# A fixed instruction order for the first layer's modulation and norms

## The chip, the cores and the metric

The kernel runs on one core of a Trainium2 chip. The metric is the device time of one execution in microseconds. The kernel before took 2765.76 us (median of three runs, 2760.23 to 2770.64). The engines are TensorE (PE; its weight loads are listed as PEld), VectorE (DVE), ScalarE (ACT), GpSimd (POOL) and SyncE (SP, which issues the DMA loads here).

## The reference, cut to what matters

Two layers of an attention and mLSTM block are followed by a second block. The change concerns the start of the first layer only. There x is the latent sequence (1024 rows of 1024) and ctx the context (256 rows of 1024):

```
sc, scc = silu(c), silu(c_ctx)
mod_x = split((sc  @ w_ada[l] + b_ada[l]), 3)     # shift, scale, gate of the latents
mod_c = split( scc @ w_ada[l] + b_ada[l] , 3)     # shift, scale, gate of the context
xn = rmsnorm(x,   norm_g) * (1 + scale_x) + shift_x
cn = rmsnorm(ctx, norm_g) * (1 + scale_c) + shift_c
aq, ak, av, ... = split(xn @ w_in)                # the same for cn
```

So before the first projection can run, 1024 x 2048 weights of w_ada (the shift and scale thirds, 8 MB in fp32) are multiplied with two vectors, and ten tiles of 128 rows are normed, transposed (features on the partitions) and modulated. The gate third comes later.

## The kernel before, in words

Rows are handled in tiles of 128: tiles 0 to 7 are x, 8 and 9 are ctx. `start` (L513) does the work described above; `phase_a` (the first projections and the attention) follows it and multiplies in the order context first (values and keys of tiles 8 and 9), then tiles 0 to 3, then 4 to 7. Its weights are loaded into the ring `rraw` (two places at the start of the arena `fa`), and split on ACT (L265) and DVE (L266).

*Rows.* `load` (L523) fetches one tile into a place of `rx`, ten places of 1024 columns in the arena `ta`. `scale` squares the row on ACT with a running sum (L469), makes the factor on DVE (L462) and POOL (L464, a power of -1/2), and multiplies in place on DVE (L531).

*Modulation vectors.* `ada(l, j)` (L421) is a generator over h, the four quarters of 256 columns; j=1 is scale, j=0 shift. `ada_rows` (L394) loads w_ada in two pieces of 512 rows (512 KB each) through a ring of five places, and multiplies them with the two vectors: 8 products of 128x256 each into one PSUM bank (L416), two hardware records a product. DVE copies the 2x256 result into the row tile `ar` (L418), of which there is one; four small products turn it into columns (L429); DVE adds b_ada into `AB` (L435), and for the scale makes (1+scale)*norm_g (L438).

*Norm.* `norm(t, h)` (L533) takes tiles t and t+1 and feature blocks 2h and 2h+1: four transposes into one PSUM buffer (L542), then the modulation straight out of PSUM into `z` (i=0 on DVE, L547; i=1 on ACT, L545), then `split` (L248): a rounded copy on ACT (L249) and the remainder on DVE (L250). There are three PSUM buffers for transposes and columns (`pt`, banks 2 to 4), and five for products (`pg`).

*What sets the order.* The lines are not issued as they are written. A scheduler places instructions on the engines by their priority (their order in the text) and its own model of time, over a block that reaches from the setup to the end of the second layer's mixers; each engine then executes its list in order. Only the last part of the program (`feed_forward`, L1990) is written in `manual_schedule`. Within such a region each engine issues the region's instructions in the order of the text; where they fall among instructions from outside the region stays with the scheduler.

Of the kernel before, what the change touches and what calls it, by code (L numbers as in the profile page):

```python
# [9 lines left out]
AF = mybir.ActivationFunctionType  # L10
ALU = mybir.AluOpType
# [176 lines left out]
FO, FS, TS = 2176, 9752, 11008  # L188


class Kernel:
# [50 lines left out]
    def mm3(self, out, lh, ll, rh, rl, start, stop):  # L242
        mm = self.nc.tensor.matmul
        mm(out, lh, rh, start=start, stop=False)  # L244
        mm(out, lh, rl, start=False, stop=False)  # L245
        mm(out, ll, rh, start=False, stop=stop)  # L246
# [58 lines left out]
    def gemm_n(self, w, kk, t, n, x=None, pg=None, ks=range(8), p=None, stop=True):  # L305

        start, p = p is None, p or (pg or self.pg).get()
        X, L = x or (self.xh, self.xl)
        g, o = (t // 4, (t % 4) * 128) if t < 8 else (2, (t - 8) * 128)
        for k in ks:  # L310
            xh, xl = X[g][:, k, o:o + 128], L[g][:, k, o:o + 128]
            h, l = w[k // kk]
            self.mm3(p[:, :n], xh, xl, h[:, k % kk], l[:, k % kk], start and k == ks[0], stop and k == ks[-1])
        if not stop:
            return p
        self.bg.step(self.rate)
        self.bg2.step()
        return p
# [5 lines left out]
    def columns(self, rows, name):  # L324

        nc = self.nc
        r = self.rraw.get([128, 128])
        o = 0
        for ap in rows:
            n = ap.shape[0]  # L330
            nc.sync.dma_start(r[o:o + n], ap)
            o += n
        p = self.pt.get()
        nc.tensor.transpose(p[:, :o], r[:o], self.ident[:o, :o])
        v = self.const([128, o], name)
        nc.vector.tensor_copy(v, p[:, :o])
        return v
# [175 lines left out]
    def start(self):  # L513

        nc, V = self.nc, self.nc.vector
        self.xh, self.xl = [None] * 3, [None] * 3
        for g in range(3):
            self.new_xn(g)
        self.phase(F32)
        rx = self.T(0, 1024, 10)  # L520
        rows = {}

        def load(t):  # L523
            src = self.A["x"][0, t * 128:(t + 1) * 128] if t < 8 else self.A["ctx"][0, (t - 8) * 128:(t - 7) * 128]
            rows[t] = x = rx.get()
            nc.sync.dma_start(x.ap, src)

        def scale(t):
            x = rows[t]
            r = self.row_rstd(x.ap, self.rny.get().ap)  # L530
            V.tensor_scalar(x.ap, x.ap, r, None, op0=ALU.mult)  # L531

        def norm(t, h):  # L533

            p = self.pt.get()
            pv = p.re("p (k n) -> p k n", k=2)
            A = self.mod(0, t)
            z = self.rnz.get([128, 2, 256])
            for i in range(2):
                for j in range(2):  # L540
                    k = 2 * h + i
                    nc.tensor.transpose(pv[:, i, j * 128:(j + 1) * 128], rows[t + j][:, k * 128:(k + 1) * 128], self.ident)  # L542
                a, b = A(k)
                if i:
                    nc.scalar.activation(z[:, i], pv[:, i], AF.Identity, scale=a, bias=b)  # L545
                else:
                    V.tensor_scalar(z[:, i], pv[:, i], a, b, op0=ALU.mult, op1=ALU.add)  # L547
            g, o = (t // 4, (t % 4) * 128) if t < 8 else (2, (t - 8) * 128)
            self.split(self.xh[g][:, 2 * h:2 * h + 2, o:o + 256], self.xl[g][:, 2 * h:2 * h + 2, o:o + 256], z.ap)

        first = [8, 9, 0, 1, 2, 3]
        for t in first:
            load(t)
        rada = Ring(self.fa, [FO + 1024, FO + 2048] + [FO + 4628 + 1024 * i for i in range(3)], 1024)
        a, b = self.ada(0, 1, rada), self.ada(0, 0, rada)
        for h in range(4):
            next(a)
            next(b)
            if h == 0:
                for t in first:  # L560
                    scale(t)
            for t in (8, 0, 2):
                norm(t, h)
        for t in range(4, 8):
            load(t)
        self.late_constants()
        for t in (4, 6):
            scale(t)
            scale(t + 1)
            for h in range(4):  # L570
                norm(t, h)


    def rings_attention(self):
# [1751 lines left out]
```

## Time and profile before

| what | us |
|---|---|
| median of three runs | 2765.76 |
| the profiled execution's own time | 2766.28 |
| its span | 2764.5 |
| PE busy | 2618.6 |
| DVE busy | 1865.3 |
| ACT busy | 1451.2 |
| first product with w_ada starts | 16.50 |
| last group of columns (L429) starts | 58.94 |
| last split of tiles 2 and 3 ends | 70.20 |

Times in the views are microseconds from the start of the span. An engine's busy time counts its instructions; a matmul's duration is longer than the distance to the next one, since matmuls are pipelined, so rates are read from the starts of consecutive groups. In the view in order of time a row is a group of equal instructions in sequence: start, duration of the group, engine, line, operation, output<-inputs, shapes, count, and in brackets the idle time before it with what ended that.

### The profile page before, as it was taken

The numbers are of one execution on the slowest core, as the hardware profiler recorded it, in microseconds if no ns is written. First come the engines' busy times: TensorE is split into PE (matmuls) and PEld (weight loads), VectorE is DVE, ScalarE is ACT, GpSimd is POOL, SyncE is SP. The second block draws the span as 40 slices with busy tenths as digits, with TensorE's granted clock in tenths as the row PEclk, the third lists the DMA queues.
The fourth block names the chain that finished last, engine by engine and source line by source line (L and its number), as shares of the span: only waits on it lengthen the run. The fifth ranks groups of instructions, "written<-read, shape, count | busy, mean of one in ns | idle before, by whom it ended". The sixth has DMA issues, their size and how long they took to land. (4 is left out here: it accounts for less than half of the span.)

```text
span 2764.5 us, 43667 instructions
## 1 busy us (share of the span) xinstructions
PE 2618.6 (95%) x16222; PEld 2273.1 (82%) x16222; DVE 1865.3 (67%) x3758; ACT 1451.2 (52%) x3035; POOL 477.6 (17%) x686
## 2 busy tenths in 40 slices
PE   7999999999899999999998989899899999999998
PEld 3888888899789887878987878778788878888887
DVE  4788756636755788765456467987844477868978
ACT  4666645646632666555455153468833644753344
POOL 0122213413300022213223030025410000000000
PEclk9999999999999999999999989999989999999999
DMA  7001111111564202022113451423242576698846
GB/s 252 25 19 49 35 49 38 55 53 47 156 199 151 81 18 59 24 61 62 44 54 115 156 171 64 128 80 96 82 126 85 184 222 214 199 326 286 282 136 213
DMA packets 302817, 324.73 MB, mean 117 GB/s; under 512 B 17968, under 2 KB 242572, under 8 KB 302348
## 3 DMA queue, kind: packets, MB, share of 16 engines
q1 hardware_dynamic: 302604, 321.95, 37.0%
q8 instruction: 127, 2.08, 0.3%
q14 instruction: 86, 0.70, 0.1%
HBM read 274.86 MB, written 47.03 MB: 116 GB/s over the span
## 5 line engine op out<-in xcount | busy, mean ns | idle before, releaser
L244 PE MATMUL psum<-xa 128*128 128x512 f32 (+2 forms) x2136 | 755.3, 354 | 11.4 <-ACT xa L249 3.5
L246 PE MATMUL psum<-xa 128*128 128x512 f32 (+2 forms) x2136 | 747.2, 350 | 5.1 <-DVE xa L2076 3.4
L245 PE MATMUL psum<-xa 128*128 128x512 f32 (+2 forms) x2136 | 749.2, 351 | 1.6 <-DVE xa L266 1.5
L244 PEld LDWEIGHTS psum<-xa 128*128 128x128 f32 x2136 | 408.0, 191 | 65.2 <-ACT xa L249 4.8
L246 PEld LDWEIGHTS psum<-xa 128*128 128x128 f32 x2136 | 407.5, 191 | 56.1 <-DVE xa L2076 5.6
L245 PEld LDWEIGHTS psum<-xa 128*128 128x128 f32 x2136 | 407.8, 191 | 50.6 <-DVE xa L266 2.2
L464 POOL TENSOR_TENSOR rsb<-rsa,half 128x1 f32<-128x1 f32 (+2 forms) x125 | 89.2, 713 | 1010.2 <-DVE rsa L462 935.7
L244 PE MATMUL psum<-xa,xg 128*128 128x256 f32 (+1 forms) x864 | 248.4, 287 | 1.8 <-DVE fa L1522 1.2
L245 PE MATMUL psum<-xa,xg 128*128 128x256 f32 (+1 forms) x864 | 246.1, 285 | 0.0
L246 PE MATMUL psum<-xa,xg 128*128 128x256 f32 (+1 forms) x864 | 245.8, 284 | 0.0
L2074 ACT ACTIVATE xa<-t816a 128x1024 fp32r<-128x1024 f32 x122 | 126.1, 1056 | 186.1 <-PE psum L245 101.8
L265 ACT ACTIVATE xa<-fa 128x1024 fp32r<-128x1024 f32 (+1 forms) x104 | 109.9, 1059 | 196.5 <-PE psum L246 98.6
L266 DVE TENSOR_TENSOR xa<-fa,xa 128x1024 fp32r<-128x1024 f32 (+1 forms) x94 | 115.3, 1229 | 135.4 <-ACT xa L265 124.9
L2076 DVE TENSOR_TENSOR xa<-t816a,xa 128x1024 fp32r<-128x1024 f32 x122 | 146.0, 1221 | 78.6 <-ACT xa L2074 78.4
L805 POOL TENSOR_SCALAR fa<-fa,esk 128x640 f32<-128x640 f32 (+2 forms) x144 | 112.1, 791 | 451.3 <-DVE esk L803 349.7
L244 PEld LDWEIGHTS psum<-xa,xg 128*128 128x128 f32 x864 | 163.9, 190 | 3.2 <-DVE fa L1522 1.6
L245 PEld LDWEIGHTS psum<-xa,xg 128*128 128x128 f32 x864 | 163.9, 190 | 0.8 <-issue 0.7
L246 PEld LDWEIGHTS psum<-xa,xg 128*128 128x128 f32 x864 | 163.6, 189 | 0.4 <-issue 0.3
L244 PE MATMUL psum<-xg,xa 128*128 128x512 f32 x376 | 153.3, 409 | 2.9 <-DVE fa L1764 1.8
L246 PE MATMUL psum<-xg,xa 128*128 128x512 f32 x376 | 152.3, 405 | 1.0 <-POOL xa L266 1.0
L245 PE MATMUL psum<-xg,xa 128*128 128x512 f32 x376 | 152.5, 405 | 0.2 <-DVE xg L250 0.2
L1008 DVE SCALAR_TENSOR_TENSOR fa<-fa,vec 128x640 f32<-128x640 f32 (+2 forms) x128 | 110.4, 869 | 52.0 <-ACT fa L1006 42.4
(511 smaller groups left out, 5880.1 us busy)
## 6 DMA issues: line engine op xcount, KB each, us to landing
t816a<-in_w_down_dram SPq DMA_DIRECT2D x72, 512.0 KB
fa<-in_w_in_dram SPq DMA_DIRECT2D x64, 512.0 KB
t816a<-in_w_up_dram SPq DMA_DIRECT2D x64, 512.0 KB
fa<-in_w_ada_dram SPq DMA_DIRECT2D x48, 512.0 KB
t816a<-hd SPq DMA_DIRECT2D x36, 512.0 KB
fa<-in_w_up_dram SPq DMA_DIRECT2D x32, 512.0 KB
fa<-in_w_out_dram SPq DMA_DIRECT2D x24, 512.0 KB
fa<-in_w_down_dram SPq DMA_DIRECT2D x24, 512.0 KB
```

The lines of the kernel that those rows point to most:

```text
L244: mm(out, lh, rh, start=start, stop=False)
L245: mm(out, lh, rl, start=False, stop=False)
L246: mm(out, ll, rh, start=False, stop=stop)
L265: self.nc.scalar.activation(h.ap, r.ap, AF.Copy)
L266: (self.nc.gpsimd if self.wpool else self.nc.vector).tensor_tensor(l.ap, r.ap, h.ap.bitcast(F32), op=ALU.subtract)
L464: self.nc.gpsimd.tensor_tensor(r, e, self.half.broadcast_to([128, m]), op=ALU.pow)
L805: nc.gpsimd.tensor_scalar(P[j][:, :nk], P[j][:, :nk], e[:, j:j + 1], 0.0, op0=ALU.mult, op1=ALU.add)
L1008: nc.vector.scalar_tensor_tensor(y, U[i][:, lo + tap:hi + tap], col(tap), y, op0=ALU.mult, op1=ALU.add)
L2074: nc.scalar.activation(h.ap, r.ap, AF.Copy)
L2076: V.tensor_tensor(l.ap, r.ap, h.ap.bitcast(F32), op=ALU.subtract)
```

## The change

The lines of `start` that prepared tiles 8, 9 and 0 to 3 go into a new function, `start_first`, written in `manual_schedule`. In it:

- w_ada's pieces (units, in the order h, then scale before shift, then the two halves of the rows) get 13 places instead of 5: four places of `rx` that tiles 4 to 7 will take later, the five of before, the two of `rraw`, and the two of `z`. Thirteen loads are issued right behind the six rows; the last three when units 4, 5 and 6 have been multiplied; then tiles 4 to 7, and at the end the late constants.
- Each pair of rows is transposed as soon as it is scaled (`turn`), and copied from PSUM back into its own place, on ACT for odd h and on DVE for even h. Tiles 8, 9, 0 and 1 are turned ahead of the first product, tiles 2 and 3 between the first four units.
- The columns of a row `ar` (`columns`) are made behind the first unit of the next row. When the shift of a quarter is there, the three pairs are modulated in place, from SBUF, and split.

`spare` is the four places of `rx` (columns 6144 on of `ta`); `products(n, p)` multiplies unit n (four products, eight records) and, for n of 4 to 6, issues one more load. Tiles 4 to 7 are handled as before, outside the region.

```diff
-        first = [8, 9, 0, 1, 2, 3]
-        for t in first:
-            load(t)
-        rada = Ring(self.fa, [FO + 1024, FO + 2048] + [FO + 4628 + 1024 * i for i in range(3)], 1024)
-        a, b = self.ada(0, 1, rada), self.ada(0, 0, rada)
-        for h in range(4):
-            next(a)
-            next(b)
-            if h == 0:
-                for t in first:
-                    scale(t)
-            for t in (8, 0, 2):
-                norm(t, h)
-        for t in range(4, 8):
-            load(t)
-        self.late_constants()
+        with self.tc.manual_schedule():
+            self.start_first(rows, load, spare)
...
+        slots = spare
+        slots.extend(Ring(self.fa, [FO + 1024, FO + 2048] + [FO + 4628 + 1024 * i for i in range(3)], 1024))
+        slots.extend(Ring(self.fa, [0, 1088, FO + 7700, FO + 8724], 1024))
+        units = [(h, j, k) for h in range(4) for j in (1, 0) for k in (0, 4)]
...
+        def turn(t, h):
+            p = self.pt.get()
+            pv = p.re("p (k n) -> p k n", k=2)
+            for i in range(2):
+                for j in range(2):
+                    k = 2 * h + i
+                    nc.tensor.transpose(pv[:, i, j * 128:(j + 1) * 128], rows[t + j][:, k * 128:(k + 1) * 128], self.ident)
+            o = both(t, h)
+            if h % 2:
+                nc.scalar.activation(o, pv, AF.Copy)
+            else:
+                V.tensor_copy(o, pv)
...
+        def columns(h, j, r):
+            t = self.pt.get()
+            for i in range(2):
+                mm(t[:, 2 * i:2 * i + 2], r[0:2, i * 128:(i + 1) * 128], self.sel[0:2, 0:2], start=True, stop=True)
...
+            V.tensor_tensor(o, t[:, 0:4].rearrange("p (k a) -> p k a", a=2), b, op=ALU.add)
+            if j == 1:
...
+                return
+            for t in (8, 0, 2):
+                A = self.mod(0, t)
+                x, g, o = both(t, h), t // 4, (t % 4) * 128
+                for i in range(2):
+                    a, b = A(2 * h + i)
+                    if i:
+                        nc.scalar.activation(x[:, i], x[:, i], AF.Identity, scale=a, bias=b)
+                    else:
+                        V.tensor_scalar(x[:, i], x[:, i], a, b, op0=ALU.mult, op1=ALU.add)
+                self.split(self.xh[g][:, 2 * h:2 * h + 2, o:o + 256], self.xl[g][:, 2 * h:2 * h + 2, o:o + 256], x)
...
+        for t in (8, 9, 0, 1, 2, 3):
+            load(t)
+        for _ in range(13):
+            fetch()
+        slots.i += 4
+        sq = [square(8), square(9)]
+        for x in sq:
+            scaled(*x)
+        sq = [square(0), square(1)]
+        for h in range(4):
+            turn(8, h)
+        for x in sq:
+            scaled(*x)
+        sq = [square(2), square(3)]
+        for h in range(4):
+            turn(0, h)
+        for x in sq:
+            scaled(*x)
+        last = None
+        for n in range(0, 16, 2):
+            h, j, _ = units[n]
+            p = self.pg.get()
+            products(n, p)
+            if n < 4:
+                turn(2, n)
+            if last:
+                columns(*last)
+            products(n + 1, p)
+            if n < 4:
+                turn(2, n + 1)
+            r = self.s([5, 256], "ar256", 1)
+            V.tensor_copy(r[0:2], p[:2, :256])
+            last = h, j, r
+            if n == 6:
+                for t in range(4, 8):
+                    load(t)
+        columns(*last)
+        self.late_constants()
```

## Rows read from the trace of the kernel before

**Rows 1.** The page: busy time of PE, share of the span, instructions

```profile
PE 2618.6 (95%) x16222; PEld 2273.1 (82%) x16222; DVE 1865.3 (67%) x3758; ACT 1451.2 (52%) x3035; POOL 477.6 (17%) x686
```

**Rows 2.** Busy time in stretches (length; each engine's busy time, count; granted clock; DMA)

```profile
16.50:59.47 42.97, 42.97 (x198) 17.54 (x198) 19.46 (x50) 15.40 (x27) 2.70 (x5) 1.00 0.80 258
59.47:70.20 10.73, 9.34 (x68) 8.01 (x68) 7.44 (x12) 6.73 (x11) 0.00 (x0) 1.00 0.62 195
```

**Rows 3.** Waits of SP and of PE: total us, times, longest

```profile
SPq L405 <- PE psum L416: 16.6, 9, 3.6
...
PE psum L416 <- DMA fa<-in_w_ada_dram: 4.5, 1, 4.5
...
PE psum L1208 <- DVE t474a L1204: 5.8, 2, 5.5
```

**Rows 4.** PE in order of time, the modulation stage

```profile
11.51 0.48 PE L542 MATMUL psum<-ident,t1a 128*128 128x128 f32 x1 [1.00 <-DVE t1a L531]
16.50 6.98 PE L416 MATMUL psum<-fa,cc 128*2 128x256 f32 x20 [4.51 <-DMA fa<-in_w_ada_dram]
...
34.83 2.32 PE L416 MATMUL psum<-fa,cc 128*2 128x256 f32 x10
37.08 0.66 PE L542 MATMUL psum<-ident,t1a 128*128 128x128 f32 x4
37.67 0.59 PE L416 MATMUL psum<-fa,cc 128*2 128x256 f32 x2
38.19 0.60 PE L429 MATMUL psum<-sel,ar 2*128 2x2 f32 x4
38.72 0.59 PE L416 MATMUL psum<-fa,cc 128*2 128x256 f32 x2
...
58.94 0.60 PE L429 MATMUL psum<-sel,ar 2*128 2x2 f32 x4
```

**Rows 5.** Stretches, transposes of L542 alone (PE busy, count; weight loads)

```profile
16.40:59.47 43.07, 7.67 (x38) 3.87 (x38) 1.00 0.80 258
...
70.20:82.00 11.80, 4.21 (x22) 2.49 (x22) 1.00 0.18 50
```

**Rows 6.** ACT in order of time

```profile
12.42 1.06 ACT L469 ACTIVATE fa<-t1a 128x1024 f32<-128x1024 f32 x1
...
41.56 0.56 ACT L545 ACTIVATE fa<-psum,AB 128x256 f32<-128x256 f32 x1 [0.22 <-ACT fa L545]
42.02 0.62 ACT L249 ACTIVATE xc<-fa 128x512 fp32r<-128x512 f32 x1
```

**Rows 7.** DVE in order of time

```profile
13.81 0.15 DVE L462 TENSOR_SCALAR rsa<-nss 128x1 f32<-128x1 f32 x1
14.69 0.75 DVE L531 TENSOR_SCALAR t1a<-t1a,rsb 128x1024 f32<-128x1024 f32 x1 [0.73 <-POOL rsb L464]
...
42.67 0.69 DVE L250 TENSOR_TENSOR xc<-fa,xc 128x512 fp32r<-128x512 f32 x1
43.28 0.68 DVE L250 TENSOR_TENSOR xa<-fa,xa 128x512 fp32r<-128x512 f32 x1
43.89 0.54 DVE L547 TENSOR_SCALAR fa<-psum,AB 128x256 f32<-128x256 f32 x1
...
58.46 0.41 DVE L418 COPY ar<-psum 2x256 f32<-2x256 f32 x1 [0.78 <-PE psum L416]
59.58 0.16 DVE L435 TENSOR_TENSOR AB<-psum,vec 128x4 f32<-128x4 f32 x1 [0.71 <-PE psum L429]
...
69.52 0.68 DVE L250 TENSOR_TENSOR xa<-fa,xa 128x512 fp32r<-128x512 f32 x1
```

**Rows 8.** Nearest shapes: a group's mean ns, and L1588's min/median/max

```profile
L606 ACT ACTIVATE fa<-psum 128x512 f32<-128x512 f32 x20 | 11.8, 592 | 14.1 <-PE psum L246 14.0
...
L1541 DVE TENSOR_SCALAR t604a<-psum,hln 128x512 f32<-128x512 f32 x4 | 3.2, 806 | 4.3 <-ACT fa L1540 4.3
...
L1588 DVE TENSOR_SCALAR fa<-fa,sst x8: 349/820/2068, 1874.0 to 1957.2; 128x256 f32<-128x256 f32 x8
```

More of the change, by code (lines that the diff above doesn't have):

```diff
@@ L519, in start @@
         self.phase(F32)
-        rx = self.T(0, 1024, 10)
+        rx, spare = self.T(0, 1024, 10), self.T(6144, 1024, 4)
         rows = {}
@@ L571, in start, with start_first, fetch, square @@
                 norm(t, h)
+    def start_first(self, rows, load, spare):
+        nc, V = self.nc, self.nc.vector
+        mm = nc.tensor.matmul
+        slots = spare
+        slots.extend(Ring(self.fa, [FO + 1024, FO + 2048] + [FO + 4628 + 1024 * i for i in range(3)], 1024))
+        slots.extend(Ring(self.fa, [0, 1088, FO + 7700, FO + 8724], 1024))
+        units = [(h, j, k) for h in range(4) for j in (1, 0) for k in (0, 4)]
+        raw = []
+        def fetch():
+            h, j, k = units[len(raw)]
+            c0 = j * 1024 + h * 256
+            r = slots.get([128, 4, 256])
+            nc.sync.dma_start(r.ap, self.A["w_ada"][0][k * 128:(k + 4) * 128, c0:c0 + 256]
+                              .rearrange("(k p) c -> p k c", p=128))
+            raw.append(r)
+        def square(t):
+            x = rows[t]
+            ss = self.s([128, 1], "nss", 4)
+            nc.scalar.activation(self.rny.get().ap, x.ap, AF.Square, accum_out=ss)
+            return x, self.rstd(ss, 1024)
+        def scaled(x, r):
+            V.tensor_scalar(x.ap, x.ap, r, None, op0=ALU.mult)
+        def both(t, h):
+            o = rows[t].slot[1]
+            assert rows[t + 1].slot[1] == o + 1024
+            return self.ta[:, o:o + 2048].rearrange("p (k n) -> p k n", k=2)[:, :, 256 * h:256 * h + 256]
+        def turn(t, h):
[10 more added lines that the diff above has]
+                V.tensor_copy(o, pv)
+        def products(n, p):
+            h, j, k0 = units[n]
+            r = raw[n]
+            for i in range(4):
+                k = k0 + i
+                mm(p[:2, :256], self.cc[:, k], r[:, i], start=(k == 0), stop=(k == 7))
+            if 4 <= n < 7:
+                fetch()
[3 more added lines that the diff above has]
+                mm(t[:, 2 * i:2 * i + 2], r[0:2, i * 128:(i + 1) * 128], self.sel[0:2, 0:2], start=True, stop=True)
+            v, ks = self.vec[0], slice(2 * h, 2 * h + 2)
+            o = self.AB[0][:, ks, 1 - j]
+            b = v[:, 8 + 8 * j + 2 * h:10 + 8 * j + 2 * h].unsqueeze(2).broadcast_to([128, 2, 2])
+            V.tensor_tensor(o, t[:, 0:4].rearrange("p (k a) -> p k a", a=2), b, op=ALU.add)
+            if j == 1:
+                g = v[:, ks].unsqueeze(2).broadcast_to([128, 2, 2])
+                V.scalar_tensor_tensor(o, o, 1.0, g, op0=ALU.add, op1=ALU.mult)
+                return
[12 more added lines that the diff above has]
+        for _ in range(13):
+            fetch()
+        slots.i += 4
[32 more added lines that the diff above has]
+        self.late_constants()
```

## The prediction

> **What bounds the kernel now.** I read the page first: TensorE (PE) is busy 95% of the span [rows 1], so a microsecond taken from PE's queue is nearly one of the span, and one taken from another engine is worth only what PE waited for it. The edit touches the first 75 us. There I read the busy time by stretches: from 16.50 to 59.47 PE has no idle time at all (42.97 us of 42.97), while DVE and ACT are busy 19.5 and 15.4 us of it [rows 2]. The waits say the same from the other side: SP waits for the products 16.6 us in nine places, while PE waits for a w_ada load once, 4.5 us, for the first [rows 3]. So this stage is bound by what stands in PE's queue from the first load's landing on, not by the loads.
>
> What stands there is read from PE's rows in order of time [rows 4]. A group of two records lasts 0.59 us and one of ten 2.32, so a record is (2.32-0.59)/8 = 0.216; two take 0.52 to the next group's start, so a change of kind costs 0.52-0.43 = 0.09. There are 128 records, two for each of 64 products. The first twenty last 6.98, where 2.32 + 10 x 0.216 = 4.48 would do: 2.5 us go to records at half speed just after PE's wait, although the granted clock reads 1.00, the 2.4 GHz level [rows 2]. So 128 x 0.216 + 2.5 = 30.1; eight groups that turn a row into columns at 0.53 = 4.2; 38 transposes [rows 5] at 0.146 (four take 0.585, from 37.08 to 37.67) = 5.6; together 39.9, and the last 3.1 are some 34 changes of kind. Ahead of it PE made only two transposes, the second at 11.51, and then stood before its first product until 16.50, though a fourth row was being scaled at 14.69 [rows 7]. The new order can make 32 of the 48 transposes of these three pairs of rows ahead of the products.
>
> **The change part by part.** All sums are against the profiled execution: 2766.28 us, with a span of 2764.5; the median of the runs is 2765.76, 0.5 lower.
>
> *Thirteen slots.* They remove SP's 16.6 us of waiting. I price that at nothing: PE never waited for loads two to sixteen. The first load still stands behind six rows on SP and lands at 16.50. SP now issues tiles 4 to 7 and the constants behind the sixteenth w_ada load, and w_in must wait until units 9 and 10 are read, as two of the new slots are its own; by the times below that is 46.3, and PE wants it at 62.0. Those 16 us are its cover; were they used up, PE would stand idle after the modulation, microsecond for microsecond.
>
> *When the first product can start.* Each engine now keeps the written order. DVE makes the factor of row 1 by 13.96, as before [rows 7], and only then copies the first transposed block. That copy, 128x512 from PSUM, isn't in the trace: its ends are 0.41 (256 columns of two partitions, 58.46) and 0.81 (a tensor_scalar of this shape, L1541) [rows 7, 8]; I take the middle, 0.6. There are three PSUM buffers, so the fourth group of tile 8 waits for it, +0.6 and +0.66 for the group; ACT copies that group, +0.59 (L606), and only then squares rows 2 and 3: +1.06 for the first, +1.39 from the second's start to its factor (12.42 to 13.81 [rows 6, 7]), +0.15. DVE's first copy of tile 0 stands behind that factor, +0.6, and the last group of tile 0 behind the copy, +0.66. The first product starts at **19.7** (19.3 to 20.1), 3.2 us after its load. So of the 4.7 us (8 x 0.585) by which eight groups leave the products' stretch, a late start takes 3.2.
>
> *The slow records.* In the trace they follow a PE that had made two transposes in 11 us. In the new order PE works some 5 of the 8 us ahead of the products; no row shows so much broken work. I take none of the 2.5 us, as the nearest row, the end of the first twenty records, has PE fast after 5 us of work; 0 and 2.5 stay as ends. The Trainium skill (TensorE: Matmul & The Clock Gate, "What's actually happening") says that the slow clock is the default state and that activity releases it; by that rule the 2.5 us go, as in the sum. The trace agrees for unbroken work; for broken work no row here shows it.
>
> *From the products to the last columns.* A unit of eight records is 1.73+0.09 = 1.82. Five units, four groups of tile 2 (0.585 each) and one column group bring the shift columns of h=0 at T = 19.7+9.1+2.3+0.5 = 31.6.
>
> *The modulation as a new wait.* Behind these columns DVE's queue holds the addition into AB and then, for each of three tiles, a tensor_scalar and the split's subtraction, which waits for ACT's copy, which waits for the tensor_scalar. Behind all six stands the copy of the next row `ar`, and behind that PE's next column group. The addition is at T+0.64 (58.94 to 59.58), 0.16 long, the first tensor_scalar at T+0.84; ACT's Identity leads to its copy 0.46 later (41.56 to 42.02), at T+1.33; the subtraction follows 0.65 after (42.02 to 42.67) at T+1.98, and DVE's next instruction 0.61 after that (43.28 to 43.89) [rows 6, 7]. The tensor_scalar now reads SBUF; with two operands that isn't in the trace. Its ends are 0.35 (the shortest L1588, SBUF, one operand [rows 8]) and 0.54 (L547, from PSUM, at 43.89 [rows 7]); I take 0.35, the row with the same memory. A further tile is then 0.61+0.35+0.65 = 1.61, the third subtraction at T+5.20, the copy of `ar` at T+5.81, PE's columns 0.48 later (58.46 to 58.94) at **T+6.29**. PE is there at T + 0.53 + 2 x 1.82 = T+4.17. It waits 2.1 us for each of h=0, 1 and 2: **6.4 us** together. Before, the scheduler ran other copies between the parts of the tiles, and no such wait shows. With 0.54 it is 2.6 each; the lower end is 0, where PE has instructions of later lines to run.
> One h is 6.29+4.17 = 10.46, so T is 42.1 and 52.5 for h=1 and 2, the scale columns of h=3 are at 58.8, its shift columns at 58.8+0.53+1.73+0.48 = **61.5**. Before: 58.94 [rows 4]. The products end 2.6 us later.
>
> *What comes back behind it.* Before, tile 2's last split ended at 69.52+0.68 = 70.20 [rows 7], with PE idle 1.4 us of 10.7; PE had made 18 transposes there (of 80 in all, 8 a tile, less 2, 38 and 22 elsewhere [rows 4, 5]) and the context's values and keys, the latter 9.34 - 18 x 0.16 - 0.26 = 6.2 us [rows 2] (0.16: a transpose in a four costs 0.146, in a pair more). 22 transposes of tiles 4 to 7 were left, 3.5 us: level at 73.7. Now that split ends at 61.5+5.20+0.69 = 67.4 and PE does the context's 6.2 us from 62.0 to 68.2. Of the 32 transposes of tiles 4 to 7 (5.1 us) so many are done by then as the scheduler puts into the 6.4 us of waits. All: PE is level at 68.2 (-5.5). None: at 73.3 (-0.4). I take half: 70.8, **-2.9 us**. The twelve new copies lie ahead of the fifth unit, and what they cost is in the start at 19.7; with that cover gone they would be 0.6 each.
> 2766.3 - 2.9 = **2763.4 us**.
>
> **The rivals.**
> 1. *Slower: DVE's queue makes the waits longer.* Scalings and splits of later lines may fall into the chain that holds `ar`: four scalings of tiles 4 to 7 (0.75), their factors (0.15) [rows 7] and two weight splits, an estimate of 1.3 each from twice the 0.69 of half the size, are 6.2 us. If all stand in it, nothing is filled and the records stay slow: -0.4+6.2+2.5 = +8.3, **2774.6**. It decides from the point where these additions exceed the 2.9 us. For: before, DVE did four scalings in this stretch. Against: DVE is idle in the second half of every h, 10.46 less some 7.
> 2. *Faster: the waits aren't there.* If `ar` is copied in time, the last columns come at 55.1, PE goes on at 55.6 and is level after 6.2+5.1 at 66.9: -6.8, **2759.5**. For: every engine but PE has slack [rows 2]. Against: the three steps of a tile are serial by their data.
> 3. *The written order isn't what sets the time.* All lines up to the second layer's end of mixers are ordered by one scheduler, which now reaches the later ones from another state. PE's waits there come in single pieces of up to 5.5 us [rows 3]; two or three gained or lost are 10 to 15 us: **2752 or 2778**. No row says which sign.
>
> **How the numbers follow.** A change of 0.5% is 13.8 us, about what a measurement of this kernel can tell from none. Forecast (-6 to +3, so 2760 to 2769): 0.55. Rival 1: 0.17; rival 2: 0.13; rival 3: 0.15, more of it on the faster side, where the stage's own sum leans. Only rival 3, alone or on top of another, passes 13.8: faster 0.11, slower 0.08, same 0.81. The range for 8 in 10 runs from just inside rival 3's gain, 2753, to rival 1's end, 2775.
>
> **What would show it.** The first product at 19.7 and not at 16.5; its records at 0.216, not twice that; gaps of 2.1 us, or transposes of tiles 4 to 7, ahead of the scale columns of h=1, 2 and 3, behind DVE's copy of `ar`; the last columns at 61 to 62; no wait for a w_ada load but the first; tile 2's last split near 67.4. The prediction is wrong if the products run from 16.5 without gaps, if PE stands after the modulation for w_in, or if the difference arises behind the first 80 us.

## The result: 0.57% slower

The changed kernel takes 2783.89 us (median of 7 runs, 2777.82 to 2788.31), the kernel before 2765.76 (7 runs, 2760.23 to 2770.64). The ratio on record, which is taken over the runs and is not the quotient of the medians, is 1.0057, interval 1.0046 to 1.0069, or 15.8 us; the medians lie 18.1 apart. Forecast were 2763.4 us and a range of 2753 to 2775. The profiled execution of the changed kernel took 2788.31 (span 2786.5), the slowest of its runs, and that of before lies near its median; so the 22.0 us between the two spans tell where time went, and their sizes are somewhat large.

From L572 on, a line of the kernel before has a number 105 higher in the changed kernel (L783 is L888). In the experiments on the changed kernel `start_first` stands at the end of the class (L2300 on), so all other lines keep the numbers of before.

The page's line on TensorE: busy time rose by 21.4 us, nearly the whole loss [rows 1]. So PE's instructions took longer; it did not stand idle much more.

```profile
PE 2640.0 (95%) x16222; PEld 2293.8 (82%) x16222; DVE 1878.2 (67%) x3764; ACT 1454.0 (52%) x3041; POOL 476.3 (17%) x686
```

I divided both spans at the same instructions: the first of L783 (first scores of layer 1), the first and last of L1032 (a mixer's state, layers 1 and 2), the last of L1374 (transposes in layer 2's projection) and the first of L1985 (the beginning of the last block). Columns: stretch, length, PE busy (count), granted clock, DMA share, GB/s. First before, then the changed kernel:

```profile
0.00:103.20 103.20, 86.01 (x421) 1.00 0.56 180
103.20:418.70 315.50, 301.47 (x1909) 0.99 0.12 37
418.70:1499.10 1080.40, 1039.88 (x7239) 0.99 0.26 74
1499.10:1664.50 165.40, 140.44 (x1013) 0.92 0.52 169
1664.50:2117.30 452.80, 418.90 (x2814) 0.95 0.29 92
2117.30:2764.50 647.20, 631.89 (x2837) 0.99 0.68 224
```

```profile
0.00:109.00 109.00, 87.94 (x420) 0.97 0.52 171
109.00:426.10 317.10, 303.55 (x1909) 0.98 0.13 36
426.10:1507.60 1081.50, 1043.21 (x7239) 0.99 0.26 74
1507.60:1674.70 167.10, 140.24 (x1003) 0.90 0.51 163
1674.70:2140.50 465.80, 433.91 (x2822) 0.93 0.29 91
2140.50:2786.50 646.00, 631.14 (x2837) 0.99 0.68 225
```

The lengths grew by 5.8, 1.6, 1.1, 1.7, **13.0** and -1.2 us. A quarter of the loss is in the stage that was edited; over half is in a stretch 1600 us later, where no line was touched. There PE's busy time grew by 15.0 and its idle time fell from 33.9 to 31.9; the granted clock went from 0.95 to 0.93. Summed from the trace's list of clock changes, the clock stood at its lower level, 1.2 GHz, for 44.4 us of this stretch before and for 68.3 in the changed kernel. Half of the 23.9 us more is 12 us, an estimate of what that costs (sixteen equal records, shown below, take 3.62 us at 1.00 and 6.57 at 0.54): nearly all of the 13.0. I call this stretch S below. It lies in the block (layer 2's projection, differential attention) that a second call of the scheduler orders: 1172 of that block's 5540 TensorE instructions stand elsewhere than before.

The edited stage, PE in order of time (start, length of the group, ..., wait before it); it answers to [rows 4]:

```profile
20.21 2.04 PE L612 MATMUL psum<-t1a,cc 128*2 128x256 f32 x8
...
32.34 0.60 PE L619 MATMUL psum<-sel,ar 2*128 2x2 f32 x4
32.88 3.62 PE L612 MATMUL psum<-fa,cc 128*2 128x256 f32 x16
39.09 0.60 PE L619 MATMUL psum<-sel,ar 2*128 2x2 f32 x4 [2.59 <-DVE ar L670]
39.62 3.62 PE L612 MATMUL psum<-fa,cc 128*2 128x256 f32 x16
43.16 0.60 PE L619 MATMUL psum<-sel,ar 2*128 2x2 f32 x4
...
51.20 0.97 PE L619 MATMUL psum<-sel,ar 2*128 2x2 f32 x4 [3.88 <-DVE rsa L462]
52.09 6.57 PE L612 MATMUL psum<-fa,cc 128*2 128x256 f32 x16
58.59 0.60 PE L619 MATMUL psum<-sel,ar 2*128 2x2 f32 x4
...
66.46 0.60 PE L619 MATMUL psum<-sel,ar 2*128 2x2 f32 x4
...
69.54 0.60 PE L619 MATMUL psum<-sel,ar 2*128 2x2 f32 x4
```

Two waits, each ahead of scale columns, and behind the second sixteen records in 6.57 us instead of 3.62. From 51.20 to 58.59 the granted clock was 0.54, the 1.2 GHz level nearly throughout. What PE waited for stands on DVE, here behind the second quarter's shift columns; the copy of `ar` (L670) is what PE needs:

```profile
47.67 0.41 DVE L636 TENSOR_SCALAR t1a<-t1a,AB 128x256 f32<-128x256 f32 x1
48.60 0.15 DVE L462 TENSOR_SCALAR rsa<-nss 128x1 f32<-128x1 f32 x1 [0.52 <-ACT fa L469]
49.47 0.76 DVE L531 TENSOR_SCALAR t1a<-t1a,rsb 128x1024 f32<-128x1024 f32 x1 [0.72 <-POOL rsb L464]
50.14 0.68 DVE L250 TENSOR_TENSOR xa<-t1a,xa 128x512 fp32r<-128x512 f32 x1
50.74 0.41 DVE L670 COPY ar<-psum 2x256 f32<-2x256 f32 x1
```

The factor and the scaling of tile 4 (L462, L531), lines of later code, stand between the third tile's modulation and its split. The factor waits for a square on ACT, and that square also sits in front of the third tile's rounded copy:

```profile
47.43 1.04 ACT L469 ACTIVATE fa<-t1a 128x1024 f32<-128x1024 f32 x1
48.38 0.19 ACT L469 ACTIVATION_READ_ACCUMULATOR fa<-t1a 128x1 f32 x1
48.47 0.61 ACT L249 ACTIVATE xa<-t1a 128x512 fp32r<-128x512 f32 x1
```

### The profile page after: what moved, and what is told of

Same layout as the page of the kernel before. It is cut to its first block, busy times and chain, and to the rows that moved or that the text cites. A ratio compares the mean times of both kernels' runs of the same rounds, so it can differ in the third digit from the quotient of the medians.

```text
span 2786.5 us, 43679 instructions
## 1 busy us (share of the span) xinstructions
PE 2640.0 (95%) x16222; PEld 2293.8 (82%) x16222; DVE 1878.2 (67%) x3764; ACT 1454.0 (52%) x3041; POOL 476.3 (17%) x686
## 5 line engine op out<-in xcount | busy, mean ns | idle before, releaser
L265 ACT ACTIVATE xa<-fa 128x1024 fp32r<-128x1024 f32 (+1 forms) x104 | 109.9, 1059 | 200.9 <-PE psum L246 97.0
```

Of the source, the lines that this page charges most:

```text
L265: self.nc.scalar.activation(h.ap, r.ap, AF.Copy)
```

## The experiments

Two theories. ORDER: the loss in S comes from the order that the scheduler gives that block in answer to a changed start. START: the whole loss arises in the first 80 us and what shows later is its echo in the clock. The order was read from the instructions of each kernel: A is that of before, B that of the changed kernel, C to G are others; one letter means the same sequence in the last 4600 of the block's 5540 TensorE instructions. "L783" is how much later than before its first instruction starts; S is the length of that stretch (both from the profile); the ratio is against runs of before on the same chip. e1, e5 and e6 rest on four timed runs, e9 and e12 on five, the other experiments on nine to twelve; S is from one profiled execution each.

| run | L783, us | order | S, us | ratio, 95% interval |
|---|---|---|---|---|
| before | 0 | A | 452.8 | |
| changed | +5.8 | B | 465.8 | 1.0057 (1.0046 to 1.0069) |
| e1 | +19.2 | G | 455.9 | 1.0063 (1.0042 to 1.0084) |
| e2 | +8.6 | C | 459.9 | 1.0043 (1.0024 to 1.0062) |
| e3 | +2.1 | C | 457.8 | 1.0011 (1.0000 to 1.0022) |
| e4 | +4.9 | D | 449.5 | 1.0002 (0.9989 to 1.0015) |
| e5 | -1.1 | B but for 25 | 462.3 | 1.0146 (1.0126 to 1.0166) |
| e6 | +6.5 | D | 457.9 | 1.0113 (1.0098 to 1.0128) |
| e7 | +0.6 | E | 451.9 | 1.0006 (0.9997 to 1.0014) |
| e8 | -1.5 | E | 454.6 | 1.0002 (0.9993 to 1.0011) |
| e9 | -0.4 | B but for 101 | 463.3 | 1.0040 (1.0028 to 1.0053) |
| e10 | 0.0 | A | 457.3 | 1.0004 (0.9995 to 1.0013) |
| e11 | +4.8 | E | 451.9 | 1.0026 (1.0015 to 1.0037) |
| e12 | +5.3 | B | 462.4 | 1.0051 (1.0037 to 1.0065) |
| e13 | -3.9 | A | 453.8 | 0.9988 (0.9978 to 0.9999) |
| e14 | -3.1 | D | 453.5 | 0.9975 (0.9966 to 0.9984) |
| e15 | -1.2 | F | 455.5 | 0.9998 (0.9988 to 1.0007) |

**e1 and e2: another order by one more load, on either kernel.** One line ahead of the block, a copy in device memory that nothing reads:

```
+ self.nc.sync.dma_start(self.sgd[0], self.A['x'][0].rearrange('(a p) n -> a p n', p=128)[:, :, 0:256])
```

> The kernel before, its start untouched, with one load of 1 MB added behind the second layer's mixers (into a buffer that is rewritten later); the scheduler then orders the differential attention nearly as in the changed kernel (326 of 5540 PE instructions stand elsewhere than there, 1167 elsewhere than in the kernel before). Theory A (some 14 of the 22 us of the two profiles arise behind 1500 us, from the other order of the last scheduled part): first L783 at 103.2 as before, start of feed-forward and total later by 8 to 16 us, 2774 to 2782. Theory B (the loss behind 1500 us follows from the late start or the clock of that run, not from the order): 2765 to 2767.

> The changed kernel with the same added load, which here gives the last scheduled part a third order (997 of 5540 PE instructions elsewhere than in the changed kernel, 1027 elsewhere than in the kernel before). Theory A: the first 80 us as in the changed kernel (second wait 3.9, last columns at 69.5, first L783 at 109.0), but the total moves by more than 3 us against 2783.9, either way. Theory B: total 2784 to 2786.

The time of e1 says nothing: the copy has no input to wait for and SP issued it at 64.00 us, in the middle of the first projection's weights (the fifth of their loads, which SP had issued by 70 us before, came at 89.82), and L783 is 19.2 us late. Its S speaks against the expectation: order G stands only 326 of 5540 instructions from B, and S is 455.9, so to be near B is not enough. In e2 S fell from 465.8 to 459.9, a first hint at ORDER, with the same flaw.

**e3: the modulation handed out.** `columns` only notes the three tiles; `modulate` does one of them after the columns and one after the copy of `ar`.

```
-            for t in (8, 0, 2):
-                ...
+            todo.extend((t, h) for t in (8, 0, 2))
...
             if last:
                 columns(*last)
+                modulate()
...
             last = h, j, r
+            modulate()
```

> The changed kernel, with one tile's modulation at a time put into the order: one behind a quarter's shift columns, one behind the copy of the next row ar, one behind the next columns. The same work, and the same order of the last scheduled part as the kernel with the added load (e2). Theory (in the written order the copy of ar stands behind three tiles' modulation on DVE, and PE's next columns behind the copy): the waits of 2.6 and 3.9 us fall under 0.7, no products at half speed behind them, last columns at 58 to 60 and not 69.5, first L783 at 98 to 102 and not 109; total 7 to 11 us under e2. Rival (the row's copy isn't what holds PE): waits and total as e2.

The two long waits went: columns follow each other every 4.08 us (35.81, 39.89, 43.97, 48.04), the last at 59.14. But L783 still came 2.1 us late. SP's queue shows a likely reason: the scheduler now put the load of the rotation table ahead of all weights of the first projection (in the changed kernel the first two of their loads were issued from 45.62 us on, ahead of that table's), and PE waited for the split of the first of them.

```profile
50.59 0.33 SPq L671 DMA_DIRECT2D fa<-in_rope_dram  x1
50.96 25.06 SPq L260 DMA_DIRECT2D fa<-in_w_in_dram  x5
```

```profile
66.22 0.58 PE L244 MATMUL psum<-xc,xa 128*128 128x256 f32 x1 [2.83 <-ACT xa L265]
```

**e4: the scalings of tiles 4 to 7 by hand, behind the last columns.**

```
         columns(*last)
+        for t in range(4, 8):
+            scale(t)
         self.late_constants()
```

> The changed kernel, with the scalings of tiles 4 to 7 taken into the written order behind the last columns, so that none can stand in the chain that holds ar. Theory: the second wait is 2.6 and not 3.9 us, as the first; if the longer wait is what slowed the 16 products behind it, these now last 3.6 and not 6.6. Third scale columns at 47 to 50; against that, tiles 4 to 7 come later: first L783 at 106 to 112. Rival (slow products have another cause than the length of the wait): they still last 6.6.

The second wait fell to that of the bare chain, and the products behind it ran at full speed:

```profile
38.28 0.60 PE L2360 MATMUL psum<-sel,ar 2*128 2x2 f32 x4 [2.60 <-DVE ar L2411]
38.82 5.30 PE L2353 MATMUL psum<-fa,cc 128*2 128x256 f32 x16
...
50.79 0.60 PE L2360 MATMUL psum<-sel,ar 2*128 2x2 f32 x4 [2.60 <-DVE ar L2411]
51.33 3.62 PE L2353 MATMUL psum<-fa,cc 128*2 128x256 f32 x16
```

So it was tile 4's scaling that lengthened that wait. What this edit does not show is that the longer wait slowed the records: here sixteen ran partly at the lower clock (5.30) behind the first wait, of 2.60, as well. At L783 the gain was only 0.9 us: beside these, eight later products took 3.32 instead of 1.89, and tiles 4 to 7 were scaled some 24 us later (75.3 to 80.3). The time is that of before nonetheless, and S is the shortest of all: the order had changed too.

**e5 and e6: orders B and D with the starts exchanged.** Two copies as in e1, now of data that layer 2's mixers write, so that they can't run early:

```
+ self.nc.sync.dma_start(self.sgd[0, 0:7], self.mix[0:7, :, 0:256]); self.nc.sync.dma_start(self.sgd[1, 0:7], self.mix[0:7, :, 256:512])
```

> The kernel before, its first 1600 us unchanged, with two small copies between buffers in device memory (0.9 MB each, nothing reads the result) put between the second layer's mixers and the block that the scheduler orders for layer 2's projection and the later attention. With them the scheduler gives that block the order of the changed kernel in all but 25 of some 5500 TensorE instructions. Theory ORDER (the changed order of that block costs about 11 us of the loss, in the differential attention from 1780 to 2065 us): line 783 still starts at 103 us, within 1 us of before, and the time is 8 to 14 us over the kernel before. Theory START (the whole loss begins in the first 80 us, and what shows later is its echo in the clock): within 3 us of the kernel before. Rival to both: the copies themselves delay the loads of layer 2's projection, then the loss stands between 1620 and 1720 us.

> The changed kernel with the same two copies at the same place; with them the scheduler gives the block the order that the run with the scalings behind the last columns had, whose delay did not grow behind 1500 us. The start is that of the changed kernel. Theory ORDER: line 783 starts 5 to 7 us later than before, line 1032 7 to 8 us later, and at the end the kernel is 4 to 9 us over before, that is 10 us or more under the changed kernel. Theory START: 17 to 23 us over before, as the changed kernel.

The copies cost some 30 us ahead of S (at the last of L1032, e5 is 28.9 late and e6 33.1), a price that neither expectation had at this place (e5's named a delay by the copies between 1620 and 1720 us); so the times say nothing. S itself went as ORDER says in e5, 462.3 with before's start and order B; e6, 457.9 with the changed start and order D, is shorter than with B but 5.1 us longer than before.

**e7 and e8: no waits and a first product at its load.** e3's edit, and tiles 0 and 1 transposed between the products; tiles 4 to 7 scaled at units 10 and 12 (e7) or behind the last columns (e8).

```
-        for h in range(4):
-            turn(0, h)
...
             if n < 4:
+                turn(0, n)
                 turn(2, n)
```

> The changed kernel with three edits in the order that is written by hand: the twelve modulations of a quarter are handed out two per half-quarter instead of all ahead of the next scale columns; the transposes of tiles 0 and 1 stand between the products instead of ahead of them; tiles 4 to 7 are scaled at products 10 and 12, by hand. If the stage's loss is the two waits ahead of the scale columns and the late first product: first product at 16 to 17 us, no wait over 1 us of TensorE on a row copy, last columns at 55 to 58 us (changed kernel 69.5), and line 783 starts 1 to 6 us before the kernel before does. If what limits the stage is the landing of the weights of the first projection (as in the run with spread modulations), line 783 starts 1 to 4 us later than before. The later block's order is a new one (neither kernel's): its price is not known, -5 to +12 us.

> As the run before it, but tiles 4 to 7 are scaled behind the last columns, which lets the scheduler put the first projection's weights ahead of the load of the rotation table. The later block has the order of the run before it. If landing of those weights limits, line 783 starts earlier than in that run, by 1 to 4 us; if the scalings on the vector engine's path limit (tiles 4 to 7 are normed last), it starts 1 to 3 us later. At the end the two differ by what they differ at line 783, within 3 us, if a block's order alone sets what it costs.

The first product started at 16.96 and 16.29, and no column waited over 0.83 us. In e7 the last columns came at 62.88, not 55 to 58: the scheduler put ten transposes and the first records of the context's projection ahead of them. In e8 they came at 55.34, and PE then waited 2.99 us for the split of the first weight (L265), which stood on ACT behind the modulation; the records behind that wait ran at the lower clock up to 64 us. Of 3.6 us at the columns 1.5 were left at L783.

**e9 to e12: the order alone.** Transposes of a constant that nothing reads, ahead of the block: they move TensorE's entry into it in the scheduler's plan, and so choose the order without touching data, loads or buffers.

```
+ dm = self.pt.get(); self.pt.i -= 1; [self.nc.tensor.transpose(dm[:, :128], self.ident, self.ident) for _ in range(56)]
```

> The kernel before with 56 transposes of a constant (nothing reads them, 0.11 us each by the rows of such transposes, 6 us) ahead of the block that the scheduler orders for layer 2's projection and the later attention. They move TensorE's entry into that block in the scheduler's plan, and it then gives the block the order of the changed kernel in all but 101 of some 5500 TensorE instructions; no data is copied, so nothing else of before is touched. Theory ORDER: line 783 as before (within 1 us), line 1374 later by the transposes (0 to 7 us), and from there to line 1985 (1664 to 2117 us of before) the delay grows by 8 to 13 us: 10 to 20 us over the kernel before. Theory START: the delay does not grow there by more than 3 us: 0 to 9 us over.

> Control: the kernel before with 20 such transposes (2.2 us), with which the scheduler keeps the order of before, instruction by instruction. Both theories: 0 to 4 us over the kernel before, all of it at the transposes; between 1664 and 2117 us the delay grows by less than 2 us. If it grows by more, the clock's state when the block begins sets that stretch and not the order.

> The changed kernel with 36 such transposes (4 us), with which the scheduler gives the block an order that stands closer to that of before (510 TensorE instructions elsewhere instead of 1172), the one that the two runs with spread modulations and late transposes had. Theory ORDER: 7 to 8 us late at line 1032, 12 to 16 us late at line 1374, and from there on the delay falls or stays (-4 to +2 us), so that it ends 9 to 17 us over before, under the changed kernel in spite of the added transposes. Theory START: it grows by 8 to 13 us as in the changed kernel, and ends 22 to 28 us over before.

> Control: the changed kernel with 20 such transposes (2.2 us); the order of the block is that of the changed kernel, instruction by instruction. Both theories: 18 to 26 us over before, the delay grows by 8 to 13 us between 1664 and 2117 us. If it grows by less than 5 us, the order does not set what that stretch costs.

S in the four, by stretches as above (e9, e10, e11, e12):

```profile
1668.30:2131.60 463.30, 426.37 (x2823) 0.94 0.30 91
```

```profile
1665.00:2122.30 457.30, 420.64 (x2813) 0.95 0.30 91
```

```profile
1670.60:2122.50 451.90, 420.79 (x2814) 0.95 0.30 92
```

```profile
1673.00:2135.40 462.40, 428.88 (x2822) 0.94 0.30 91
```

Before's start with order B: S is 10.5 us longer than before, of that 7.5 PE busy time. The changed start with order E: S is 0.9 us shorter than before, though L783 is 4.8 us late. Both controls keep their side: A 457.3, B 462.4. e10's growth of 4.5 us misses its bound of 2, beyond which, by its expectation, not the order but the state of the clock would set the stretch. S does move within one order, by 4.5 us with A and by 8.4 with D (449.5 to 457.9). But the four values with B (462.3 to 465.8) lie above all thirteen others (449.5 to 459.9). The bounds of S move with the order as well (with B nine more PE records lie in it than with A); taken from the last of L1032 to the first of L1985, the four with B are still the longest, 629.1 to 632.9 us against 617.0 to 626.8. So ORDER holds as a shift of some 9 us between means, not as a fixed price, and START, by which S would follow the start, falls. In the timed runs e11 lies under e12 by 0.25%, 6.8 us, though it has 16 transposes more. Their totals, some 7 and 14 us over before, are both below what was expected (9 to 17 and 18 to 26).

**e13 and e14: a start without waits, and orders that cost nothing.** e8 with the first weights' split by hand at the last pair of products; in e13 that of the second weight as well, and both remainders on GpSimd.

```
+            if n == 14:
+                self.early.append(self.weights([self.A["w_in"][0][:, C_AV:C_AV + 128]], 8, 128))
             products(n + 1, p)
...
-        wv, wk, wq = colw(C_AV), colw(C_AK), None
+        wv, wk, wq = (self.early.pop(0) if self.early else colw(C_AV)), colw(C_AK), None
```

> The run with spread modulations, late transposes and scalings behind the last columns, and in addition the first two weights of the first projection are split by hand (the high part on ScalarE at the last pair of products, the rest on GpSimd), so that TensorE does not wait 3.0 us for the split at 58.9. The scheduler gives the later block the order of before, instruction by instruction. If the loss at the start was waits and the lower clock behind them: line 783 starts 4 to 9 us earlier than in the kernel before (that run: 1.5 earlier), the stretch from the last of line 1374 to the first of line 1985 is 451 to 458 us as with that order before, and the time is 2 to 8 us under the kernel before. If the stage is bound by something else (2.4 us of GpSimd for a split, the norms of tiles 4 to 7): line 783 within 2 us of before and the time the same.

> As the run before it, but only the first weight is split by hand, and on the vector engine; the later block gets the order that took 449.5 us in that stretch in the run with the scalings alone moved behind the last columns. Line 783 starts 2 to 7 us earlier than before; that stretch takes 448 to 455 us if the order sets it, 456 to 466 if it does not; the time is 2 to 9 us under the kernel before.

Both are a little faster than before: e13 takes 2763.34 us and e14 2761.27, against 2768.42 of before on that chip; the changed kernel did not run there. In e13, with before's order, L783 comes 3.9 us earlier, just under the 4 to 9 that were expected, and the time is 0.12% (3.3 us, interval 0.3 to 6.1) less. e3 against e2, both with order C, has L783 6.5 us earlier and 0.32% (8.9 us) less time; e8 against e7, with order E, 2.1 and 0.04% (1.1). So without a change of order the start's gain reaches the end, about one to one as far as these three pairs can tell. e14's PE shows what is left of the wait for the split:

```profile
54.92 0.38 PE L244 MATMUL psum<-xc,xa 128*128 128x256 f32 x1 [0.73 <-ACT xa L265]
55.14 0.28 PE L245 MATMUL psum<-xc,xa 128*128 128x256 f32 x1
56.18 0.39 PE L246 MATMUL psum<-xc,xa 128*128 128x256 f32 x1 [0.76 <-DVE xa L266]
```

**e15: the slots alone,** nine places for w_ada's loads in the kernel before.

```
-        rx = self.T(0, 1024, 10)
+        rx, spare = self.T(0, 1024, 10), self.T(6144, 1024, 4)
...
-        rada = Ring(...)
+        rada = spare; rada.extend(Ring(...))
```

> The kernel before with 9 slots for the loads of w_ada instead of 5 and nothing else: the part of the change that spares the waits of the DMA queue. The products run back to back from 16.50 to 59.47 us before, so the first stage is the same to 1 us (line 783 at 102 to 104 us). The scheduler orders the later block in a way that no other run had (996 TensorE instructions elsewhere): if the order sets what the stretch from the last of line 1374 to the first of line 1985 costs, it is some value of its own between 449 and 466 us, and the time follows it: from 3 us under to 13 us over the kernel before; if not, within 3 us of before.

L783 came 1.2 us earlier and the time is the same: nine of the thirteen slots are worth nothing that can be measured, as priced.

## Why the prediction was wrong

*What held.* The first product at 20.21 (19.7 was forecast, 20.1 the latest); its eight records in 2.04 us (1.89 at full speed); the shift columns at 32.34 (31.6); no wait for w_ada. So nearly none of the 2.5 us of slow records stayed.

*Why no slow records stayed was in part luck.* The granted clock of 1.00 that the prediction read beside its slow records shows nothing: the trace's list of clock changes begins at 21.6 us before, with a rise to the higher level, and ahead of its first entry the column reads 1.00. In the changed kernel the list begins at 20.6, so the slow stretch was spent on the transposes (sixteen in 4.21 us; in e12, with the same written start and a list that begins at 15.5, eleven of them take 1.42), and the first product came so late that it was nearly over. In e8 the same fifteen transposes stand ahead, the first product came at 16.29, and its eight records were slow, up to the first entry at 19.8:

```profile
16.29 3.57 PE L2353 MATMUL psum<-t1a,cc 128*2 128x256 f32 x8 [0.94 <-DMA t1a<-in_w_ada_dram]
```

The rule of the Trainium skill (TensorE: Matmul & The Clock Gate, "What's actually happening"), that the slow clock is the default state and that activity releases it, agrees with these rows: in each of the three kernels the first records are slow and the later ones fast. That the transposes ahead would be enough, which the prediction took from its nearest row, e8 does not bear out.

*The new wait, right in kind.* The first is 2.59 us, where 2.1 was worked out. Together the two that came are 6.5, the forecast for three 6.4. The third, ahead of h=3, is filled by transposes of tiles 4 to 7 and the context's first records, all but 1.4 us.

*The step that failed in the stage* is the modulation's period of 10.46 us. From h=1's shift columns to h=2's it took 15.43 (43.16 to 58.59), 5.0 more. Of these, 1.3 are the longer wait (3.88 against 2.59), which by e4 is tile 4's scaling in the chain; 0.5 the chain itself, which even without it took 6.75 (32.34 to 39.09) and not 6.29; and 3.2 the columns and sixteen records at the lower clock. For these the sum had no term: it priced slow records behind the first load alone. The last columns came at 69.54 instead of 61.5, tile 2's last split ended at 77.37 instead of 67.4 (before 70.20 [rows 7]). That is rival 1; of its mechanism e4 shows the scaling, while the lower clock is seen behind the wait and not shown to follow from the wait's length. It was priced at most at +8.3; L783 was 5.8 late. Also wrong: half of the transposes of tiles 4 to 7 were to fill the waits; these rows were fetched only from 36.94 on and the first was scaled at 49.47, so PE did none of them before 62.67. So "-2.9" was +5.8.

*The step that failed in the sum* is the end of it: that what happens behind 74 us stays as it was. That was rival 3's door, at 0.15 and with more weight on the faster side, and reckoned for the lines up to the end of the second layer's mixers, in single waits of PE. There little was added (+2.7 us from L783 to the last of L1032). The loss came one block later, from a second call of the scheduler, as 13.0 us (9 between the means with order B, 463.5, and order A, 454.6), and not in waits but as longer busy time. The start's 5.8 and these 9 make up 14.8 of the 15.8 us on record. The text had named this as what would make it wrong: a difference behind the first 80 us. Its chances did not fit together either: 0.19 for changes that only rival 3 could bring, which itself had 0.15.

*What stays open.* Why order B makes PE's records longer. By the estimate above, the price in the changed kernel's profile is paid mostly in the clock: in S it stood at 1.2 GHz for 51.2 to 68.3 us with B and for 37.5 to 44.4 with A (34.1 to 54.6 with the others, so the clock alone does not set B apart). What in B brings it down more often is not shown, as no run changed single instructions of that order. How much of a late start reaches the end when the order changes as well (e4, e11) is not settled either.

## What to carry to other kernels

Where a scheduler orders later code, an edit's price is not read from the edited stage alone: compare the order of the untouched blocks first, and if it moved, try the edit with several orders (a few idle instructions ahead of the block choose one) before you judge it. In an order written by hand, a small copy that TensorE waits for must not stand behind a serial chain of two engines; hand the chain out, one piece behind each copy, and keep the scheduler's later lines out of it. When a wait is gone, look for the next one (here the landing and the split of the next weights) before you count the gain.

## What the runs showed of the hardware that was not expected

The same wait of PE can be followed by either clock. The changed kernel, e2, e6, e11 and e12 have the same written start. After their first wait, of 2.59 or 2.60 us, the next sixteen records took 3.62 us in the changed kernel and in e11, but 5.30 in e2, e6 and e12; e4 has both behind two waits of 2.60 (5.30 at a granted clock of 0.67, and 3.62). After their second wait, of 3.88 or 3.89 us, they took 5.28 to 6.57 in all five, most in the profile of the changed kernel. So the length of a short wait alone does not tell which.

Nor does the work ahead. The first records of w_ada, behind the same fifteen transposes, ran at full speed in e14 (eight in 1.89, after a wait of 0.41 us), but took 2.33 in e13 (after 0.25) and 3.57 in e8 (after 0.94). The trace's list of clock changes begins, with the higher level, at 15.0 us in e14, 16.4 in e13 and 19.8 in e8, and the slow records are those ahead of these times.
